# The queries' chain of the second layer, recorded at high priority, in a two-layer decoder trunk on one core

## The chip, the cores and the metric

The kernel runs on one core of one Trainium2 chip. The metric is device time in microseconds (us), the median of several runs. Of the engines, PE multiplies matrices (its weight loads are shown apart, as PEld), DVE and ACT work on vectors, POOL and SP here mostly issue transfers.

## The reference, cut to what matters

The input is a sequence of 256 tokens with 2048 features in float32. Two layers follow each other, each a pre-normalised mixer with a gate and a residual add. The first is a "forgetting" attention with 32 heads. The second, in which the change lies, is sliding-window attention with 32 query heads on 4 key heads, a rotation of the first 16 of each head's 64 features, and a sink per head:

```python
p = h @ swa_w_in[j]
q = p[..., :WQ].reshape(B, S, SWA_Q_HEADS, SWA_HEAD_DIM)
k = p[..., WQ:WQ + WK].reshape(B, S, SWA_KV_HEADS, SWA_HEAD_DIM)
v = p[..., WQ + WK:WQ + 2 * WK].reshape(B, S, SWA_KV_HEADS, SWA_HEAD_DIM)
gate = p[..., WQ + 2 * WK:]
q = partial_rope(q, pos)
k = partial_rope(k, pos)
y = swa_attention(q, k, v, swa_sinks[j])     # window 128, softmax with a sink
...
y = y * jax.nn.silu(gate)
x = x + y @ w_out
```

## The kernel before, in words

**Units and weights.** Every projection is cut into units of 256 output columns. A unit's weights come in four parts. A part is fetched by SP's queue into a raw tile `wraw` (four buffers) and split into a high and a low half, so that the product keeps nearly the full precision: ACT casts the high half (line 221) and DVE subtracts it from the raw part (line 222), both into one of five tiles `w`. PE takes a part in 16 matmuls, eight wide ones (512 columns) and eight narrow ones, 64 for a unit. Parts are taken in pairs (wide, wide, narrow, narrow), and up to five parts are loaded ahead, so a tile that PE has freed holds the part that is due three to four parts later.

**Groups.** The second layer has a unit for the keys, one for the values, and then eight groups 0 to 7, each of a query unit and a gate unit. When a unit's last matmul has been recorded, its consumer is recorded. `SwaGroup.q` is the query consumer. It has ten steps: `low_half` copies half of the accumulator on ACT (tile `half`, line 294); DVE adds the other half (`rot_t`, line 828), shuffles the result into `rot` with a mask load before it (line 830), multiplies both by the rotation's tables (lines 833, 834) and adds them (line 877); `stack_q` then splits the queries as the weights are split and lays the halves above each other (tile named `q` in the profile): two casts on ACT (line 365) and two subtractions on DVE (line 366). The tiles `rot_t`, `rot` and `q` have one buffer each.

The gate consumer is the longer one: `half` again, two DVE steps (lines 323, 324), three activations (311 to 313), a DVE step (314), one more activation (317) and a product (318). Its result is read when the group's attention output is multiplied by it.

**Attention stages.** They are not written where they run. `after` puts them down for a later count of matmul steps, and `tick`, which counts, records them between the matmuls at a high priority:

```python
def tick():
    clock[0] += 1
    for fn in due.pop(clock[0], ()):
        with tc.high_priority(HP):      # HP = 200
            fn()
```

For the second layer `SWA_DUE = ((35, 64), (52, 80), 90)`, counted from the query consumer, where one unit is 32 steps: the scores of the group's first head pair at 35, those of the second at 52, the transposition of the softmax (DVE, tile `turned`, line 466) at 64 and 80, and, in odd groups, the products with the values for two groups (tiles `psy`, `psy_s`) at 90. So the first scores of a group come just behind its gate unit, among the first matmuls of the next query unit. A score stage is six matmuls into `ps_s` that read `q`, the row maximum on DVE (lines 388, 449, 453, 888 to 891), four exponentials on ACT (line 336) and four scalings on ACT (line 355).

**What sets the order.** The matmuls stay in the order in which they are recorded. For the other engines a planner in the framework lays the order down when the program is built: whenever an engine is free in its plan, it takes, of the instructions whose inputs are there, the one with the smallest number. The number is the place in the recording; inside `tc.high_priority(200)` it is 200 smaller. From a group's query consumer to the next there are 223 recorded instructions, or 293 where the value products lie between. The order in each engine's queue is then fixed: on the chip an instruction waits behind those before it in its queue, whatever has become ready.

Before the change the stages of `tick` have the smaller numbers, and the query consumer has plain ones. So has everything else: the weight splits, the gate consumer.

Of the kernel before, what the change touches and what calls it, by code (L numbers as in the profile page):

```python
# [25 lines left out]
HP = 200  # L26
# [32 lines left out]
def trunk(  # L59
# [16 lines left out]
    nc = tc.nc  # L76
# [215 lines left out]
    def low_half(ps):  # L292
        s = work.tile([P, 2, S], F32, tag="half", name="half", bufs=HALVES)
        nc.scalar.copy(s, ps[:, :, S : 2 * S])  # L294
        return s

    def each(row):

        return row.unsqueeze(1).to_broadcast([P, 2, S])
# [61 lines left out]
    def stack_q(t):  # L361

        q2 = work.tile([P, 2, 2, S], F32R, tag="q2", name="q2", bufs=QBUFS)
        for hh, (w, other) in enumerate(((TOP, BOTTOM), (BOTTOM, TOP))):
            nc.scalar.copy(q2[w, :, hh, :], t[w])
            nc.vector.tensor_sub(q2[other, :, hh, :], t[w], q2[w, :, hh, :].bitcast(F32))  # L366
        return [q2[:, j] for j in range(2)]
# [185 lines left out]
    class FoxGroup(Group):  # L553
# [5 lines left out]
        def q(self, ps):  # L559
            t = fox.tile([P, 2, S], F32, tag="q", name="q", bufs=1)  # L560
            nc.vector.tensor_add(t, ps[:, :, 0:S], low_half(ps))
            nc.vector.tensor_mul(t, t, each(state["r08"][:, 0:S]))
            self.qT = stack_q(t)
# [260 lines left out]
    def rotate(ps):  # L824

        rr = state["rr"]
        t = swa.tile([P, 2, S], F32, tag="rot_t", name="rot_t", bufs=1)
        nc.vector.tensor_add(t, ps[:, :, 0:S], low_half(ps))
        u = swa.tile([P, 2, S], F32, tag="rot", name="rot", bufs=1)
        nc.vector.stream_shuffle(  # L830
            u.rearrange("p c s -> p (c s)"), t.rearrange("p c s -> p (c s)"), PARTNER
        )
        nc.vector.tensor_mul(t, t, each(rr[:, 0, :]))  # L833
        nc.vector.tensor_mul(u, u, each(rr[:, 1, :]))
        return t, u
# [33 lines left out]
    class SwaGroup(Group):  # L869
# [3 lines left out]
            self.u = u  # L873

        def q(self, ps):
            t, u = rotate(ps)
            nc.vector.tensor_add(t, t, u)  # L877
            self.qT = stack_q(t)

            self.attend(2 * self.u, SWA_DUE, (self.other, self) if self.u % 2 else (), True)  # L880

# [96 lines left out]
    def load_x(q):  # L978
        a, b = XP[q]

        eng = nc.scalar if q == 1 else nc.sync
        eng.dma_start(out=xT[:, a:b, :], in_=xt_d[:, a:b, :])
# [172 lines left out]
```

## Time and profile before

| | before |
|---|---|
| time, median of 3 runs | 829.42 us (829.41 to 829.52) |
| the profiled execution's own time | 828.36 us |
| its span in the profile | 826.6 us, 13821 instructions |
| PE busy | 809.6 us (98%) |
| PEld busy | 707.6 us (86%) |
| DVE busy | 633.8 us (77%) |
| ACT busy | 523.5 us (63%) |
| HBM read | 148.55 MB, 183 GB/s over the span |

The span runs from the first to the last instruction that the profiler saw on the core. A share is busy time over the span. In a timeline, a row is a start, a length, an engine, a line of the kernel, the operation, `out<-in`, the shapes and a count; a bracket holds the time the engine stood idle before the row and what ended that. Rows of the same kind that follow each other are merged into one. The second layer's groups lie between about 513 and 720 us.

### The profile page before, as it was taken

To read this page: it belongs to the slowest core of one execution; us is meant where nothing else is said; L and a number is where in the kernel's file an instruction comes from. 1 tells how busy PE (TensorE), PEld (TensorE's weight loads), DVE (VectorE), ACT (ScalarE), POOL (GpSimd) and SP (SyncE) were. 2 spreads that over 40 slices of the span, in tenths; PEclk is the share of its full clock that TensorE was granted. 3 is DMA by queue.
4 is the path that set the end of the run, shared out by engine and by line. 5 is a ranking of instruction groups with operands and counts; after the bars stand their busy time and mean duration, and the time that the engine had idled before them with its cause. 6 is when DMAs were issued, how large, how long until landed. Compare 5 with 4: busy or idle time off the path is not lost.

```text
span 826.6 us, 13821 instructions
## 1 busy us (share of the span) xinstructions
PE 809.6 (98%) x5090; PEld 707.6 (86%) x5090; DVE 633.8 (77%) x1181; ACT 523.5 (63%) x962; POOL 61.5 (7%) x102
## 2 busy tenths in 40 slices
PE   9999999999999999999999999999989989899996
PEld 7988888888888888888888888888878878788886
DVE  6988866887578866778659668699988899975655
ACT  7776674766657566575646556478667866765642
POOL 1012100100001010010003110200000000001210
PEclk9999999999999999999999999999989999999998
DMA  9766665566656565555555665955554345644642
GB/s 297 255 210 223 198 198 186 172 191 199 195 168 211 171 208 188 182 186 176 170 179 181 201 193 175 249 161 175 161 176 152 130 153 164 192 146 144 201 131 103
DMA packets 47731, 151.85 MB, mean 184 GB/s; under 512 B 5696, under 2 KB 7392, under 8 KB 47664
## 3 DMA queue, kind: packets, MB, share of 16 engines
q1 hardware_dynamic: 44640, 141.71, 53.2%
q0 software_dynamic: 1872, 7.67, 3.7%
q10 hardware_dynamic: 1152, 1.60, 0.5%
q8 instruction: 40, 0.66, 0.3%
q14 instruction: 27, 0.22, 0.1%
HBM read 148.55 MB, written 2.41 MB: 183 GB/s over the span
## 4 chain that ended last, share of the span: by engine, by line
PE 80%; DVE 8%; ACT 7%; issue 3%; DMA 2%; DVEq 0%; SPq 0%; ACTq 0%
PE acc L80 74%; DVE w L222 2%; PE ps_s L80 2%; ACT w L221 2%; PE psy L80 2%; ACT st L336 2%; PE pt L83 1%; ACT st L355 1%; DMA wraw<-in_swa_in_dram 1%; DVE q L366 1%; DVE gt L323 1%; DVE rot_t L877 0%; DVE turned L466 0%; DMA wraw<-in_vf_dram 0%; DVE rot_t L833 0%
## 5 line engine op out<-in xcount | busy, mean ns | idle before, releaser
L80 PE MATMUL acc<-xs,w 128*128 128x512 f32 (+1 forms) x2624 | 475.5, 339 | 0.0
L80 PEld LDWEIGHTS acc<-xs,w 128*128 128x128 f32 x2624 | 405.3, 190 | 53.3 <-issue 0.7
L222 DVE TENSOR_TENSOR w<-wraw,w 128x1024 fp32r<-128x1024 f32 (+4 forms) x277 | 324.6, 1180 | 114.1 <-ACT w L221 112.5
L221 ACT CAST w<-wraw 128x1024 fp32r<-128x1024 f32 (+4 forms) x277 | 276.0, 1008 | 141.4 <-PE acc L80 107.6
L80 PE MATMUL acc<-ys,w 128*128 128x512 f32 (+1 forms) x960 | 171.0, 340 | 0.0
L80 PEld LDWEIGHTS acc<-ys,w 128*128 128x128 f32 x960 | 148.7, 191 | 20.7 <-issue 0.5
L80 PE MATMUL acc<-w,xs 128*128 128x512 f32 (+2 forms) x512 | 110.3, 363 | 0.7 <-ACT w L221 0.7
L80 PEld LDWEIGHTS acc<-w,xs 128*128 128x128 f32 x512 | 86.0, 189 | 15.2 <-ACT w L221 1.2
L336 ACT ACTIVATE st<-st,mx 128x128 f32<-128x128 f32 (+1 forms) x128 | 56.6, 444 | 17.6 <-DVE mx L631 17.1
L80 PE MATMUL ps_s<-kk,q 128*128 128x256 f32 (+1 forms) x160 | 33.3, 321 | 7.4 <-DVE q L366 7.1
L294 ACT COPY half<-acc 128x512 f32<-128x512 f32 x56 | 32.6, 583 | 9.6 <-PE acc L80 9.1
L80 PEld LDWEIGHTS ps_s<-kk,q 128*128 128x128 f32 x160 | 25.2, 196 | 12.1 <-DVE q L366 9.0
L710 POOL TENSOR_TENSOR acc<-acc,sq 128x256 f32<-128x256 f32 x28 | 23.7, 848 | 89.0 <-ACT sq L704 87.9
L388 DVE CUSTOM_DVE_ANT_0 st<-ps_s,st 128x128 f32<-128x128 f32 (+1 forms) x96 | 28.2, 331 | 0.7
L311 ACT ACTIVATE gate_e<-gt 128x512 f32<-128x512 f32 x16 | 10.1, 628 | 24.7 <-DVE gt L324 24.7
L618 POOL DMA_DIRECT2D bc<-negc_d x16 | 8.9, 554 | 214.6 <-DVE st L413 143.8
L422 ACT COPY pts<-pt 128x384 f32<-128x384 f32 x32 | 15.2, 473 | 14.2 <-PE pt L83 13.8
L336 ACT ACTIVATION_READ_ACCUMULATOR st<-st,mx 128x1 f32 x128 | 24.1, 188 | 0.0
L355 ACT ACTIVATE st<-st,rl 128x128 f32<-128x128 f32 x64 | 23.9, 445 | 0.1
L155 ACT ACTIVATE xs<-xT,g_sb 128x256 fp32r<-128x256 f32 x32 | 15.5, 502 | 13.0 <-DVE xT L690 12.0
L708 POOL COPY acc<-sq 128x256 f32<-128x256 f32 x2 | 1.4, 675 | 298.9 <-ACT sq L704 298.9
L124 POOL TENSOR_SCALAR_AFFINE_SELECT bc<-bc 128x256 f32<-128x256 f32 x32 | 18.0, 585 | 73.8 <-DMA bc<-negc_d 73.8
(146 smaller groups left out, 579.1 us busy)
## 6 DMA issues: line engine op xcount, KB each, us to landing
wraw<-in_fox_in_dram SPq DMA_DIRECT2D x96, 512.0 KB, 4.5
wraw<-in_swa_in_dram SPq DMA_DIRECT2D x72, 512.0 KB, 4.7
wraw<-in_fox_out_dram SPq DMA_DIRECT2D x32, 512.0 KB, 3.9
wraw<-in_swa_out_dram SPq DMA_DIRECT2D x32, 512.0 KB, 4.4
wraw<-in_fox_in_dram SPq DMA_DIRECT2D x54, 256.0 KB, 4.4
bc<-negc_d POOLq DMA_DIRECT2D x16, 384.0 KB, 5.4
wraw<-in_vf_dram SPq DMA_DIRECT2D x4, 288.0 KB, 5.1
xT<-in_xt_dram SPq DMA_DIRECT2D x2, 512.0 KB, 8.4
```

What stands on the lines that cost most here:

```text
L80: tc.keep_in_program_order(nc.tensor.matmul(*args, **kw))
L124: return nc.gpsimd.affine_select(out=ap, in_=ap, compare_op=ALU.is_ge, fill=NEG, base=base, pattern=pattern, channel_multiplier=mult,)
L155: nc.scalar.activation(xs[:, kt, 0, :], xT[:, kt, :], AF.Copy, scale=g)
L221: state["split"] = nc.scalar.copy(high, raw)
L222: nc.vector.tensor_tensor(out=low, in0=raw, in1=high.bitcast(F32), op=ALU.subtract)
L294: nc.scalar.copy(s, ps[:, :, S : 2 * S])
L311: nc.scalar.activation(e, z, AF.Abs)
L336: nc.scalar.activation(st[:, hh, rng], st[:, hh, rng], AF.Exp, bias=nm[:, qb, hh : hh + 1], accum_out=l[:, qb, hh : hh + 1],)
L355: nc.scalar.mul(st[:, hh, rng], st[:, hh, rng], rl[:, qb, hh : hh + 1])
L388: nc.vector.tensor_tensor_reduce(out=st, in0=high, in1=st, scale=self.scale, scalar=LOWEST, op0=ALU.add, op1=ALU.max, accum_out=self.mx[:, ...
L422: nc.scalar.copy(group.new_pts(self.j, hh)[:, hh, self.j, :], pt[:, 0 : 3 * P])
L710: nc.gpsimd.tensor_add(sums[0], sums[0], s)
```

## The change

The ten steps of `SwaGroup.q` are recorded inside `tc.high_priority(HP)`, the priority that the attention stages have. The call of `attend`, which puts the stages down for later, stays outside. What is computed does not change, nor the number of instructions. `rotate` is also called for the keys, in `swa_k`; that call is as it was.

```diff
         def q(self, ps):
-            t, u = rotate(ps)
-            nc.vector.tensor_add(t, t, u)
-            self.qT = stack_q(t)
+            with tc.high_priority(HP):
+                t, u = rotate(ps)
+                nc.vector.tensor_add(t, t, u)
+                self.qT = stack_q(t)
 
             self.attend(2 * self.u, SWA_DUE, (self.other, self) if self.u % 2 else (), True)
```

## The prediction

> **What bounds the kernel now.** I read the page first (how busy each engine is), then the table of waits for the stretch in which the second layer's queries are made (500 to 745 us), then TensorE's own timeline there, and last the timeline of ACT and DVE around one of the gaps found. The page's busy line says that PE is the engine to save time on:
>
> ```profile
> PE 809.6 (98%) x5090; PEld 707.6 (86%) x5090; DVE 633.8 (77%) x1181; ACT 523.5 (63%) x962; POOL 61.5 (7%) x102
> ```
>
> So only time in which PE stands still, or runs below its clock, can be won. The table of waits (who waited for whom, us in total, times, longest) names one such wait in the second layer, and shows that the splitting of weights is not one: ACT's cast waits for PE to free a tile, and no row of the table has PE wait for `w`.
>
> ```profile
> ACT w L221 <- PE acc L80: 29.7, 17, 4.0
> PEld ps_s L80 <- DVE q L366: 9.0, 6, 3.2
> PE ps_s L80 <- DVE q L366: 7.1, 5, 2.7
> ```
>
> `ps_s<-kk,q` are the score products of a group; `q L366` is the last step of the chain that the change moves. PE's timeline (start, length, count, and in brackets the idle time before) shows which groups wait:
>
> ```profile
> 537.42 6.21 PE L80 MATMUL acc<-xs,w 128*128 128x512 f32 x34
> ...
> 567.92 13.61 PE L80 MATMUL acc<-xs,w 128*128 128x512 f32 x76
> ...
> 587.32 6.21 PE L80 MATMUL acc<-xs,w 128*128 128x512 f32 x34
> ...
> 594.08 16.44 PE L80 MATMUL acc<-xs,w 128*128 128x512 f32 x94
> 613.25 2.15 PE L80 MATMUL ps_s<-kk,q 128*128 128x256 f32 x6 [2.73 <-DVE q L366]
> 615.20 8.22 PE L80 MATMUL acc<-xs,w 128*128 128x512 f32 x34
> ...
> 643.38 6.21 PE L80 MATMUL acc<-xs,w 128*128 128x512 f32 x34
> ...
> 668.32 0.38 PE L80 MATMUL ps_s<-kk,q 128*128 128x256 f32 x1 [1.75 <-DVE q L366]
> ...
> 695.90 6.21 PE L80 MATMUL acc<-xs,w 128*128 128x512 f32 x34
> ...
> 720.86 0.38 PE L80 MATMUL ps_s<-kk,q 128*128 128x256 f32 x1 [1.99 <-DVE q L366]
> ...
> 730.35 13.72 PE L80 MATMUL acc<-ys,w 128*128 128x512 f32 x76
> ```
>
> These are groups 3, 5 and 7. What each costs is read from the repeating work. The rows at 537.42, 587.32, 643.38 and 695.90 are the same point (just behind the first scores) of groups 0, 2, 4 and 6. From 0 to 2 it takes 49.90 us, and no wait for `q` lies between; from 2 to 4 it takes 56.06, from 4 to 6 52.52. So groups 3 and 5 cost 6.16 and 2.62 us. For group 7 the second scores end the comparison: 537.42 to 567.92 is 30.50 us (group 0 to group 1), 695.90 to 730.35 is 34.45, which is 3.95 more. Together 12.73 us.
>
> That is more than the idle time, and the windows (last columns: granted clock, DMA share, GB/s) say why:
>
> ```profile
> 613.20:616.00 2.80, 2.61 (x8) 2.19 (x9) 2.74 (x4) 1.24 (x2) 0.00 (x0) 0.50 0.69 233
> 666.00:670.00 4.00, 1.91 (x11) 1.25 (x10) 3.91 (x6) 2.08 (x4) 0.00 (x0) 1.00 0.78 253
> 720.80:724.00 3.20, 2.81 (x11) 2.42 (x12) 3.10 (x8) 1.60 (x3) 0.00 (x0) 0.68 0.57 219
> ```
>
> Behind the gaps of groups 3 and 7 PE is granted 0.50 and 0.68 of its clock, behind that of group 5 all of it; 34 matmuls take 8.22 us at 615.20 where they take 6.21 elsewhere. A gap that goes takes its slow stretch with it. The Trainium skill, "TensorE: Matmul & The Clock Gate", section "Why this matters for your kernels", asks for no idle gaps over about 3 us between bursts of matmuls; by that rule groups 5 and 7, whose gaps are shorter, would cost their idle time alone, and the sum would be smaller by what group 7 lost to its clock. The trace agrees for group 5 (1.00) and not for group 7 (0.68 behind an idle time of 1.99); the comparison of periods contains what was really lost, so the sum goes by it.
>
> **The change part by part.** Group 3 shows what the chain waits behind, in the timeline of ACT and DVE:
>
> ```profile
> 598.42 1.04 ACT L221 CAST w<-wraw 128x1024 fp32r<-128x1024 f32 x1
> ...
> 599.36 0.40 ACT L336 ACTIVATE st<-st,mx 128x128 f32<-128x128 f32 x1
> ...
> 601.23 0.62 ACT L317 ACTIVATE gate_e<-gate_e 128x512 f32<-128x512 f32 x1
> ...
> 601.83 1.50 ACT L355 ACTIVATE st<-st,rl 128x128 f32<-128x128 f32 x4
> ...
> 603.23 0.56 ACT L294 COPY half<-acc 128x512 f32<-128x512 f32 x1
> 603.35 0.98 DVE L466 STREAM_TRANSPOSE turned<-st 128x768 f32<-128x768 f32 x1 [0.78 <-ACT st L355]
> 603.69 2.95 ACT L221 CAST w<-wraw 128x1024 fp32r<-128x1024 f32 x3
> 604.26 0.65 DVE L828 TENSOR_TENSOR rot_t<-acc,half 128x512 f32<-128x512 f32 x1
> 604.83 1.21 DVE L222 TENSOR_TENSOR w<-wraw,w 128x1024 fp32r<-128x1024 f32 x1
> ...
> 605.97 0.73 DVE L830 STREAM_SHUFFLE rot<-rot_t 128x512 f32<-128x512 f32 x1
> 606.60 1.20 DVE L222 TENSOR_TENSOR w<-wraw,w 128x1024 fp32r<-128x1024 f32 x1
> 607.73 0.68 DVE L833 TENSOR_TENSOR rot_t<-rot_t,rope_c 128x512 f32<-128x512 f32 x1
> ...
> 608.33 0.68 DVE L834 TENSOR_TENSOR rot<-rot,rope_c 128x512 f32<-128x512 f32 x1
> 608.93 1.21 DVE L222 TENSOR_TENSOR w<-wraw,w 128x1024 fp32r<-128x1024 f32 x1
> 609.17 0.58 ACT L294 COPY half<-acc 128x512 f32<-128x512 f32 x1
> ...
> 610.07 0.68 DVE L877 TENSOR_TENSOR rot_t<-rot_t,rot 128x512 f32<-128x512 f32 x1
> ...
> 610.78 1.26 ACT L365 CAST q<-rot_t 64x512 fp32r<-64x512 f32 x2
> 611.80 0.68 DVE L323 TENSOR_TENSOR gt<-acc,half 128x512 f32<-128x512 f32 x1
> 612.51 1.41 DVE L366 TENSOR_TENSOR q<-rot_t,q 64x512 fp32r<-64x512 f32 x2
> ```
>
> No instruction is added or removed. Per group ten move forward in the ordering: on ACT the copy `half` and two casts (0.56 + 1.26 = 1.82 us), on DVE add, shuffle with its mask load, two products, add and two subtractions (0.65 + 0.73 + 0.68 + 0.68 + 0.68 + 1.41 = 4.83 us). None is a DMA, and POOL's queue is passed by none. SP's queue is touched only through DVE: a raw buffer is free when its subtraction (L222) is done.
>
> *The start.* The copy at 609.17 is that of the gate unit and starts as that unit ends. At 6.21/34 = 0.183 us a matmul the 64 matmuls of the gate unit before it began at about 597.4 (an estimate), so `half` of the q unit was ready about then and ran at 603.23, 5.8 us late. In front of it on ACT: a weight cast, four exponentials, L317 and the scaling L355. Of these L317 is a gate step, recorded with no lift some 130 instructions earlier, which a lift of 200 overtakes. Exponentials and L355 are lifted themselves and recorded first, so they keep their lead. The cast at 598.42 may already have been taken when the q unit ended. So bounds of the gain at the start: 0 (the exponentials and L355 block it as now) and 603.23 - 598.42 = 4.8 us. I take the slot of L317, 603.23 - 601.23 = 2.0 us, because it alone is left by rank; DVE is idle 0.78 us before 603.35, so the add follows at once.
>
> *The way.* From `half` to the last subtraction the chain takes 613.92 - 603.23 = 10.7 us, of which its own work is about 6. Between its steps DVE takes weight subtractions of 1.2 us, three before L877. These already rank behind the chain; they slip in where a step's result isn't yet out, so priority alone doesn't forbid them. But they follow casts that ran at 603.69, behind `half`; with the chain 2 us earlier and L317 and L355 behind the copy, the first cast is some 0.6 us later than now, and the chain is 2.6 us further on. Bounds: 0 and 3 x 1.2 = 3.6 us. I take two of three, 2.4 us, and nothing for the gate's L323 (0.68).
>
> *The sum.* PE was ready for the scores at 594.08 + 16.44 = 610.52 and could start at 613.25. Start and way, 2.0 + 2.4 = 4.4 us, cover the 2.73 of group 3, the 1.75 of group 5 and the 1.99 of group 7, with about 1.7 us to spare in the worst. So all 12.73 us go, of which I keep back 0.4 us for a second subtraction that comes as PE arrives. The profiled execution took 828.36 us (span 826.6) and would take about 816.0; the median of the runs is 1.06 above that execution, so 817.0.
>
> *What is pushed back.* L317 and L318 end a gate that is read only after the value products, half a group later or more: nothing. The weight splits are what could cost. A w tile freed by PE is due again after three to four parts of 16 matmuls, 8.8 to 11.7 us at 0.183 each. The cast at 603.69 fills a tile freed at about 597.4; its subtraction ends at 606.04 and is due at 609.1, 3.0 us later. That is the cover, and a pushed subtraction delays the raw buffer's next DMA alike. If the whole chain (4.83) went before it, PE would wait 1.8 us; I expect less than 3.0 of pushing, since steps and subtractions go on alternating, and take 0. In the other groups, where `q` is in time, the chain moves up by at most a subtraction and gains nothing. The transposition `turned` of the group before now ranks behind the chain; in group 4 the nearest rows are
>
> ```profile
> 635.36 0.97 DVE L466 STREAM_TRANSPOSE turned<-st 128x768 f32<-128x768 f32 x1
> ...
> 637.51 0.34 PE L80 MATMUL psy_s<-turned,vr 32*64 32x128 f32 x4
> ```
>
> with 637.51 - 636.33 = 1.18 us of cover. One chain step ahead of it (0.7) fits, both subtractions (1.41) would cost 0.2 us a time, three times: 0.6 us at most, taken as 0.
>
> **The rivals.** *In part.* The start gains its 2.0 us and the way nothing, or the way one subtraction and the start nothing. The first leaves 0.73 us in group 3 and 0.3 us or so in each of the three from the second subtraction: about 2 of 12.73, so 818.7. The second leaves 1.5, 0.55 and 0.8 us of idle, and behind the largest perhaps a lower clock again (group 3 lost 6.16 - 2.73 = 3.4 us beyond its idle time before): 4 to 6 us left, 820.7 to 822.7. For it speaks that the subtractions in between already rank lower; against it, that their casts ran at 603.69, behind the copy.
>
> *No change.* The exponentials and L355 outrank the copy before and after, and L317 goes where it goes: order and time stay, 829.4. Against it: L317 carries no lift, and at 601.23 the copy had been ready for some 3.8 us.
>
> *Slower, by weights.* The chain goes whole before the split that is due first, and PE waits 4.83 - 3.0 = 1.8 us for `w` in each of the eight groups: 14.6 us against 12.73 won, so about 831.3. It decides from 1.6 us a group on, that is when the chain pushes the split by 4.6 us or more. For it: DVE stands between two rows of the fence above for no more than 0.78 us. Against it: ACT waits for PE to free tiles 17 times in this stretch, never PE for a split.
>
> **How the numbers follow.** All gone or nearly: 0.56, 817.0, by itself 815.8 to 818.3. In part: 0.25, 818.7 to 822.7. No change: 0.08. Slower by weights, or by weights with the gaps kept: 0.11. A measurement of this kernel can tell about 0.2%, 1.7 us, from no change. The first two are faster by more, 0.81; 0.08 the same; 0.11 slower. The range holds the first two with the upper end of the second and an estimate's error on either side, 815.4 to 823.5, and leaves out 0.19.
>
> **What would show it.** The waits of PE for `q L366` at groups 3, 5 and 7 gone, and periods from group 2 to 4 and 4 to 6 near 49.9 us; `half` ahead of L317 on ACT; fewer than three weight subtractions between L828 and L877; a clock of 1.00 through 613 to 724. Wrong: the same order on ACT and DVE; rows of PE waiting for `w` or `turned`; or PE idle as long for another releaser at the same places.

## The result and the profile after

The changed kernel takes 818.3 us (median of 4 runs, 816.71 to 819.01) against 829.47 us before; the ratio of the two means is 0.9857, 95% interval 0.9836 to 0.9878, so 1.4% faster. The forecast was 817.0, range 815.4 to 823.5. The profiled execution took 819.01 us, the longest of the four, with a span of 817.2 us.

PE is busy for less time and for a larger share:

```profile
PE 805.2 (99%) x5090; PEld 703.5 (86%) x5090; DVE 631.6 (77%) x1181; ACT 522.6 (64%) x962; POOL 61.2 (7%) x102
```

In the table of waits of the same stretch, 500 to 745 us, the wait for the queries has shrunk from 9.0 and 7.1 us to 0.8 and 0.3. A small new one has come, for the product at L951 (L950 before; lines behind the edit are one higher). No row of the table has PE or PEld wait for `w`:

```profile
ACT w L221 <- PE acc L80: 15.0, 9, 3.6
...
PEld ps_s L80 <- DVE q L366: 0.8, 2, 0.5
...
PE ps_s L80 <- DVE gt L951: 0.7, 1, 0.7
...
PE ps_s L80 <- DVE q L366: 0.3, 1, 0.3
```

PE's timeline has the points from which the prediction worked out its periods:

```profile
539.43 6.21 PE L80 MATMUL acc<-xs,w 128*128 128x512 f32 x34
...
589.34 6.21 PE L80 MATMUL acc<-xs,w 128*128 128x512 f32 x34
...
612.38 0.88 PE L80 MATMUL ps_s<-kk,q 128*128 128x256 f32 x6
613.09 6.21 PE L80 MATMUL acc<-xs,w 128*128 128x512 f32 x34
...
639.25 6.21 PE L80 MATMUL acc<-xs,w 128*128 128x512 f32 x34
...
689.56 0.95 PE L80 MATMUL ps_s<-kk,q 128*128 128x256 f32 x6 [0.69 <-DVE gt L951]
690.35 6.21 PE L80 MATMUL acc<-xs,w 128*128 128x512 f32 x34
...
713.76 0.86 PE L80 MATMUL ps_s<-kk,q 128*128 128x256 f32 x5 [0.31 <-DVE q L366]
...
721.01 13.72 PE L80 MATMUL acc<-ys,w 128*128 128x512 f32 x76
```

From group 0 to 2 it takes 49.91 us as before, from 2 to 4 49.91 (56.06 before), from 4 to 6 51.10 (52.52), and the last piece 30.66 (34.45). Against 49.90, 49.90 and 30.50 that is a loss of 1.37 us where it was 12.73. Group 3 has no gap left, and its 34 matmuls behind the scores take 6.21 us where they took 8.22. The granted clock (third number from the end) is 1.00 behind the scores of groups 3 and 7, where it was 0.50 and 0.68:

```profile
613.00:640.00 27.00, 27.00 (x267) 23.93 (x266) 24.81 (x58) 18.38 (x43) 0.00 (x0) 1.00 0.57 179
...
713.00:724.00 11.00, 10.69 (x66) 9.43 (x65) 10.44 (x28) 6.73 (x17) 0.00 (x0) 1.00 0.71 232
```

So 11.4 us were won here. The two spans differ by only 9.4 us, because the point at 539.43 was at 537.42 before: 2.0 us went earlier, in the first layer and the keys and values, where the order of instructions is the same. Over the runs the medians differ by 11.2.

Why the gap of group 3 is gone is seen on ACT and DVE:

```profile
600.48 1.03 ACT L221 CAST w<-wraw 128x1024 fp32r<-128x1024 f32 x1
...
601.42 0.40 ACT L336 ACTIVATE st<-st,mx 128x128 f32<-128x128 f32 x1
...
603.28 0.56 ACT L294 COPY half<-acc 128x512 f32<-128x512 f32 x1
...
603.88 1.50 ACT L355 ACTIVATE st<-st,rl 128x128 f32<-128x128 f32 x4
603.88 0.69 DVE L828 TENSOR_TENSOR rot_t<-acc,half 128x512 f32<-128x512 f32 x1
...
604.61 0.75 DVE L830 STREAM_SHUFFLE rot<-rot_t 128x512 f32<-128x512 f32 x1
605.28 0.62 ACT L317 ACTIVATE gate_e<-gate_e 128x512 f32<-128x512 f32 x1
605.40 0.98 DVE L466 STREAM_TRANSPOSE turned<-st 128x768 f32<-128x768 f32 x1
605.80 2.94 ACT L221 CAST w<-wraw 128x1024 fp32r<-128x1024 f32 x3
606.31 0.65 DVE L833 TENSOR_TENSOR rot_t<-rot_t,rope_c 128x512 f32<-128x512 f32 x1
606.88 0.68 DVE L834 TENSOR_TENSOR rot<-rot,rope_c 128x512 f32<-128x512 f32 x1
607.48 0.68 DVE L318 TENSOR_TENSOR gt<-gt,gate_e 128x512 f32<-128x512 f32 x1
608.08 0.68 DVE L878 TENSOR_TENSOR rot_t<-rot_t,rot 128x512 f32<-128x512 f32 x1
608.68 1.22 DVE L222 TENSOR_TENSOR w<-wraw,w 128x1024 fp32r<-128x1024 f32 x1
608.80 1.26 ACT L365 CAST q<-rot_t 64x512 fp32r<-64x512 f32 x2
609.93 1.40 DVE L366 TENSOR_TENSOR q<-rot_t,q 64x512 fp32r<-64x512 f32 x2
```

The copy now stands right behind the exponentials, in the place that L317 had, and L355 and L317 follow it. The three casts come behind L317, so between the first add (L828) and the second (L878) there is no weight subtraction at all where there were three. One stands behind L878, as before. The chain ends at 611.33, before PE wants the scores at 612.38.

The copy came 2 us late for an instruction of 0.62 us because L317 did not block alone. When L317 took ACT at 601.23, the scalings L355, which rank above the copy, still waited for their reciprocal. By the end of L317 at 601.85 that was there, and they went first too. The row before the change, on DVE:

```profile
601.55 0.18 DVE L352 RECIPROCAL rl<-l 128x4 f32<-128x4 f32 x1
```

### The profile page after: what moved, and what is told of

It is laid out like the page before. It is cut to its first block, busy times and chain, and to the rows that moved or that the text cites. A ratio compares the mean times of both kernels' runs of the same rounds, so it can differ in the third digit from the quotient of the medians.

```text
span 817.2 us, 13823 instructions
## 1 busy us (share of the span) xinstructions
PE 805.2 (99%) x5090; PEld 703.5 (86%) x5090; DVE 631.6 (77%) x1181; ACT 522.6 (64%) x962; POOL 61.2 (7%) x102
## 4 chain that ended last, share of the span: by engine, by line
PE 80%; DVE 7%; ACT 5%; DMA 3%; issue 3%; SPq 1%; DVEq 0%; ACTq 0%
PE acc L80 74%; DVE w L222 3%; DMA wraw<-in_fox_in_dram 2%; PE ps_s L80 2%; PE psy L80 2%; ACT w L221 1%; PE pt L83 1%; ACT st L336 1%; ACT st L355 1%; DMA wraw<-in_vf_dram 1%; SPq L208 0%; DVE ssq L995 0%; DVE turned L466 0%; DVE q L366 0%; DVE xs L156 0%
## 5 line engine op out<-in xcount | busy, mean ns | idle before, releaser
L509 ACT CAST ys<-gt 128x512 fp32r<-128x512 f32 x16 | 9.5, 619 | 24.4 <-DVE gt L955 16.2
L355 ACT ACTIVATE st<-st,rl 128x128 f32<-128x128 f32 x64 | 23.9, 445 | 1.3 <-DVE rl L352 1.1
```

The lines of the kernel that those rows point to most:

```text
L355: nc.scalar.mul(st[:, hh, rng], st[:, hh, rng], rl[:, qb, hh : hh + 1])
```

## The experiments

The theory: the gain begins at one place, on ACT, where the copy overtakes the gate's L317; the weight subtractions then drop out of the chain because their casts come later (theory 1). The rival: what counts is that the DVE steps and the casts of the chain rank above the weight splits (theory 2). The measure is the loss of the three periods, with 12.73 us before. Read in the same way from each kernel's PE timeline, with the period from group 0 to 2 beside it. Each ratio is taken to runs of the kernel before that were measured beside that kernel (medians of 829.30 to 830.18 us):

| kernel | time, us | ratio to before (95%) | 0 to 2 | 2 to 4 | 4 to 6 | 6 to 7 | loss of the three |
|---|---|---|---|---|---|---|---|
| before | 829.42 | | 49.90 | 56.06 | 52.52 | 34.45 | 12.73 |
| the change | 818.3 | 0.9857 (0.9836 to 0.9878) | 49.91 | 49.91 | 51.10 | 30.66 | 1.37 |
| copy alone | 820.56 | 0.9872 (0.9849 to 0.9896) | 51.00 | 50.14 | 51.20 | 31.58 | 2.62 |
| all but the copy | 828.81 | 0.9984 (0.9968 to 0.9999) | 49.91 | 52.54 | 54.10 | 34.50 | 10.84 |
| lift of 77 | 829.01 | 0.9978 (0.9960 to 0.9995) | 50.54 | 55.85 | 52.52 | 34.48 | 12.55 |
| odd groups alone | 822.13 | 0.9890 (0.9872 to 0.9908) | 49.91 | 51.63 | 52.42 | 30.65 | 4.40 |
| gate set back | 818.89 | 0.9870 (0.9841 to 0.9898) | 49.91 | 49.90 | 50.98 | 31.62 | 2.20 |
| lift of 400 | 818.32 | 0.9858 (0.9832 to 0.9885) | 51.29 | 49.91 | 49.90 | 30.10 | -0.39 |
| values at 86 | 818.22 | 0.9859 (0.9835 to 0.9884) | 49.93 | 50.92 | 50.89 | 30.26 | 1.77 |
| change again | 818.15 | 0.9859 (0.9836 to 0.9883) | 49.90 | 50.01 | 51.19 | 30.68 | 1.58 |
| 200, then 400 | 816.49 | 0.9840 (0.9823 to 0.9856) | 49.91 | 49.91 | 49.92 | 30.09 | -0.38 |
| change, third | 819.24 | 0.9871 (0.9850 to 0.9891) | 50.01 | 50.80 | 51.17 | 30.69 | 2.36 |

The loss is below zero with the lift of 400 since the piece from group 6 to the scores of group 7 takes 30.10 us undisturbed, 0.40 less than the piece from group 0 to 1 that stood in for it. By that, group 7 had cost 4.35 us before, not 3.95. By the intervals of the ratios, the runs from 0.9857 to 0.9872 can't be told from each other; what differs between them is read from the profiles.

**The copy alone.**

Against the kernel before, with `rotate` taking the copy as an argument:

```diff
         def q(self, ps):
-            t, u = rotate(ps)
+            with tc.high_priority(HP):
+                half = low_half(ps)
+            t, u = rotate(ps, half)
             nc.vector.tensor_add(t, t, u)
             self.qT = stack_q(t)
```

> Only the copy `half` of the query consumer is lifted by 200, the other nine steps are plain. Theory 1 (the gain begins where the copy overtakes the gate's L317 on ACT, and the weight subtractions fall out of the way because their casts come later): the copy runs right behind the exponentials of the group before, the waits for q L366 in groups 3, 5 and 7 shrink to under 0.7 us each, and of the 12.73 us that the three groups lost against the undisturbed period at most 3 are left; about 818 to 820 us. Theory 2 (the lift of the DVE steps and of the casts over the weight splits carries it): 9 us or more of the 12.73 stay, 826 us or more.

2.62 of 12.73 us are left, as theory 1 expects. The time, 820.56 us, is a little above its range, since another 1.1 us are lost in the period before, which the measure leaves out. In group 3 the copy stands ahead of L317, as with the full change:

```profile
603.00 0.56 ACT L294 COPY half<-acc 128x512 f32<-128x512 f32 x1
...
605.00 0.62 ACT L317 ACTIVATE gate_e<-gate_e 128x512 f32<-128x512 f32 x1
```

The chain ends at 612.19, after 9.2 us, where the full change takes 8.05: the other nine steps' lift is worth about 1.1 us of the chain in group 3. Its absence shows as small waits for `q` (at most 0.62 us of PE at a time) in groups 1, 5 and 7.

**All but the copy.** The same edit the other way round: `half` recorded plain, the rest lifted.

> The nine steps behind the copy are lifted by 200, the copy itself is plain. Theory 1: the copy stays behind L317 and L355 on ACT, DVE still meets the casts' subtractions, and 6 to 12 us of the 12.73 stay: 823 to 829 us. Theory 2: 3 us or less stay, 818 to 820 us.

10.84 us are left, as theory 1 expects; theory 2 falls. PE waits at the same three places. In groups 3, 5 and 7 DVE takes the steps and the weight subtractions in the same order as before: the lift of the nine steps moved nothing there. Only in group 3 is PE's wait shorter, 1.76 us against 2.73, because the copy ran 1.0 us earlier behind the point of group 2 (603.60 - 588.69 = 14.91 us against 15.91). This run also has the clock's part by itself (PE's timeline, then the windows with the granted clock as the third number from the end):

```profile
613.65 0.39 PE L80 MATMUL ps_s<-kk,q 128*128 128x256 f32 x1 [1.76 <-DVE q L366]
...
615.07 6.21 PE L80 MATMUL acc<-xs,w 128*128 128x512 f32 x34
...
666.18 0.39 PE L80 MATMUL ps_s<-kk,q 128*128 128x256 f32 x1 [1.76 <-DVE q L366]
...
667.60 7.79 PE L80 MATMUL acc<-xs,w 128*128 128x512 f32 x34
```

```profile
613.60:617.00 3.40, 3.02 (x15) 2.49 (x16) 3.31 (x9) 1.81 (x3) 0.00 (x0) 1.00 0.53 201
...
666.20:671.00 4.80, 4.47 (x15) 3.49 (x16) 4.70 (x15) 1.90 (x3) 0.00 (x0) 0.65 0.57 169
```

Behind the same idle time, 1.76 us, the 34 matmuls took 6.21 us in group 3 and 1.58 us more in group 5. The period with group 3 lost 2.64 us, that with group 5 4.20.

**A lift of 77.** `high_priority(77)` in place of `high_priority(HP)`. In the order as the planner lays it down, 77 leaves the copy behind the gate's L317 and 80 (not run) carries it past. So by rank the gate lies some 78 instructions back, not 130 as the prediction counted. That would fit a count in which instructions recorded inside a lift are left out, which no run here tests.

> All ten steps are lifted, by 77 in place of 200. That is the largest lift that leaves them behind the gate steps of the group before; the weight splits recorded last and the transposition recorded later are overtaken. Theory 1: the copy in the odd groups stays where it was, all three waits stay, 10 to 13 us of the 12.73 are left: 826 to 830 us. Theory 2 (ranking above the weight splits is what counts): 3 us or less are left, 818 to 820 us.

12.55 us of 12.73 are left, with 2.56 us of idle PE in group 3. There the order on ACT and on DVE is that of before, with L317 and the scalings ahead of the copy:

```profile
602.98 0.61 ACT L317 ACTIVATE gate_e<-gate_e 128x512 f32<-128x512 f32 x1
...
604.98 0.56 ACT L294 COPY half<-acc 128x512 f32<-128x512 f32 x1
```

A higher rank that stops short of the gate wins next to nothing (0.18 us); the gate is what had to be overtaken.

**The gate set back.** To test the blocker from the other side, the query consumer is as before the change, and the gate's last two steps rank 100 lower in the second layer (`...` stands for lines left out; behind the edit, line numbers are one higher, so L317 is L318 here):

```diff
-    def silu(z):
+    def silu(z, late=0):
...
-        nc.scalar.activation(e, e, AF.Exp)
-        nc.vector.tensor_mul(z, z, e)
+        with tc.high_priority(late):
+            nc.scalar.activation(e, e, AF.Exp)
+            nc.vector.tensor_mul(z, z, e)
...
-            silu(g)
+            silu(g, -100 if isinstance(group, SwaGroup) else 0)
```

> The query consumer as before the change, plain. Instead the last two gate steps of the second layer (the activation at L317 and the product at L318 of the listings) are set back by 100 in the ordering, so that they rank behind the copy. Theory 1 (L317 is what the copy has to overtake): the copy runs right behind the exponentials of the group before, as in the changed kernel, and at most 4 us of the 12.73 are left, like the 2.6 of the run with the copy lifted alone; 819 to 822 us. Rival (the chain needs a rank of its own): 9 us or more are left, 826 us or more.

Without any lift of the queries 10.5 of the 12.73 us are gone, at 818.89 us. In group 3 the copy stands ahead of the activation:

```profile
601.59 0.57 ACT L294 COPY half<-acc 128x512 f32<-128x512 f32 x1
...
604.53 0.62 ACT L318 ACTIVATE gate_e<-gate_e 128x512 f32<-128x512 f32 x1
```

That shows L317 as the instruction behind which the copy, and with it PE, had waited. The product L318 of the listings was set back too, but it runs on DVE, where it had ended at 602.57 in group 3, ahead of the copy.

**Odd groups alone.** `high_priority(HP if self.u % 2 else 0)`.

> Lifted by 200 in groups 1, 3, 5 and 7 alone; groups 0, 2, 4 and 6 plain. Theory 1: the three waits sit in odd groups and go as with the full change, about 818 us. The new wait of 0.69 us in group 6 (scores behind the product L951, which stands behind two weight subtractions on DVE) comes from group 6's own lift and goes: the period from group 4 to 6 falls from 51.10 to 49.9 us, about 1 us less than the full change. Rival: that wait comes from elsewhere (the PE being early) and stays, then 51 us as before it.

The odd groups' waits go, as expected. The second half of the expectation fails, and so does its rival: the wait for the score bank grows, and there are two of them.

```profile
639.58 0.95 PE L80 MATMUL ps_s<-kk,q 128*128 128x256 f32 x6 [1.49 <-DVE gt L951]
...
692.00 0.95 PE L80 MATMUL ps_s<-kk,q 128*128 128x256 f32 x6 [1.93 <-DVE gt L951]
```

The scores and the value products share the one bank pair of `ps_s`; L951 reads it for the gate. DVE's timeline at group 6 shows L951 directly behind the plain query chain, which ends late:

```profile
688.32 0.70 DVE L878 TENSOR_TENSOR rot_t<-rot_t,rot 128x512 f32<-128x512 f32 x1
...
689.70 1.39 DVE L366 TENSOR_TENSOR q<-rot_t,q 64x512 fp32r<-64x512 f32 x2 [0.69 <-ACT q L365]
691.10 0.76 DVE L951 TENSOR_TENSOR gt<-psy_s,gt 128x256 f32<-128x256 f32 x2
```

Before the change the even groups were just as plain and had no wait for the bank. What differs is that PE no longer stalls in the odd groups. The likely reading, which is argued and not shown, is that the stalls had given DVE the time to keep up. Once they are gone the lift of the even groups is worth 1.73 + 2.52 - 1.20 = 3.05 us.

**A lift of 400.** `high_priority(400)`.

> All ten steps lifted by 400 in place of 200, so that they also overtake the exponentials and scalings of the group before. Theory 1: the start comes up to 2 us earlier still, but PE waits for q by only 0.3 us a time after the change, so there is nothing left to win there: what the three periods lose stays between 0.5 and 2.5 us (1.37 with a lift of 200), 817 to 820 us. Rival a: earlier is better, the loss goes to about 0. Rival b: the transposition `turned` comes late and PE waits for it at the value products, a loss above 3 us, 821 us or more.

From group 2 on nothing is lost (rival a), so the 0.5 to 2.5 us of the theory were too much. But 1.39 us go on the way to group 2, where PE stands idle 1.27 us before the value products (`psy_s`) at 585.25. The profile names no releaser there; the transposition that they read ends at 585.16, behind steps of the lifted chain (rival b, in one place). The time is that of the change.

**The values earlier.** `SWA_DUE = ((35, 64), (52, 80), 86)`.

> The change, and the value products recorded 4 steps earlier (86 in place of 90, about 1.5 us). Theory: the score bank is read by the product L951 before the next scores want it, the wait in group 6 (0.69 us of PE) goes, and the loss falls from 1.37 to under 0.5 us: about 1 us less than the changed kernel, 817.3 us. Rival: the transposition is not yet done at the earlier place, PE waits there instead, and the loss is 1.4 us or more.

The rival held, with 1.77 us lost: the bank wait is gone, and PE waits for the transposition instead, in groups 4 and 6.

```profile
631.95 0.34 PE L80 MATMUL psy_s<-turned,vr 32*64 32x128 f32 x4 [0.92 <-DVE turned L466]
...
682.85 0.34 PE L80 MATMUL psy_s<-turned,vr 32*64 32x128 f32 x4 [0.89 <-DVE turned L466]
```

**The change again.**

> The changed kernel once more, beside the others. About 818 us; the three periods lose 1.0 to 1.7 us again; the point behind the first scores of group 0 lies anywhere from 537 to 540 us, as it has varied in the profiles so far with the same order of instructions before it.

1.58 us and 818.15 us: the remainder repeats.

**200 up to group 2, then 400.** `high_priority(2 * HP if self.u > 2 else HP)`.

> A lift of 200 in groups 0 to 2, as in the change, and of 400 from group 3 on. With 400 everywhere the periods from group 2 on lost nothing, but 1.39 us went at the value products in group 2, where PE waited for the transposition; with 200 everywhere groups 0 to 2 lost nothing. Theory: each keeps what it had, the three periods lose 0.3 us or less together and the period from group 0 to 2 is 49.9 us; 1.3 us less than the change in the profile, about 817 us, which the medians can hardly tell from the change. Rival: the plan of the later groups hangs on that of the earlier ones, and a loss of 1 us or more shows up at another place.

The first three groups and the last five each keep the better of the two. PE's timeline has no idle time before any score:

```profile
539.32 6.21 PE L80 MATMUL acc<-xs,w 128*128 128x512 f32 x34
...
589.23 6.21 PE L80 MATMUL acc<-xs,w 128*128 128x512 f32 x34
...
639.14 6.21 PE L80 MATMUL acc<-xs,w 128*128 128x512 f32 x34
...
689.06 6.21 PE L80 MATMUL acc<-xs,w 128*128 128x512 f32 x34
...
719.15 13.72 PE L80 MATMUL acc<-ys,w 128*128 128x512 f32 x76
```

At 816.49 us (815.6 to 817.17) it beats the kernel before, and it is 2.7 us below the change, which was run beside it on the same chip. Part of that is that the change lost more in this run than in its others (2.36 us against 1.37 and 1.58).

**The change, a third time, beside that.**

> The changed kernel beside it, with more rounds: 818.2 us, and 1.4 to 1.6 us lost in the three periods.

That run took 819.24 us (817.89 to 819.72), a little above the forecast, and lost 2.36 us, since the bank wait was there in group 4 too (0.65 us).

## Why the prediction was right, point by point

*Where the time is lost.* Three waits in groups 3, 5 and 7, 12.73 us by the periods. Right in place; the undisturbed last piece shows that group 7's term was 0.40 us too small.

*The start.* Forecast: the copy takes the slot of L317, 2.0 us. Measured from the period's point, it ran 603.23 - 587.32 = 15.91 us behind it before and 603.28 - 589.34 = 13.94 after: 1.97 us. The lift of 77 and the gate set back show that this slot is the cause. The working was off by its count of instructions (130 for some 78); a lift of 200 passes both. The working also said that L355 keeps its lead. It falls behind the copy, since its reciprocal is not there yet when the copy takes the slot, and the 2.0 us are L317 and L355 together.

*The way.* Forecast: two of three subtractions fall out, 2.4 us. The chain shortened from 10.69 to 8.05 us, 2.64. All three left the stretch before L878, and so did the gate's L323 (0.68), for which nothing was taken. In their place the transposition (0.98) and the gate's L318 (0.68) slip in between the steps. So the reason was right, casts that come later, but that 2.64 is so near to 2.4 is partly luck.

*The sum.* Forecast 12.73 less 0.4. Measured 11.36 by the same periods. The step that failed is "In the other groups ... the chain moves up by at most a subtraction and gains nothing", taken with no cost there. The period from group 4 to 6 loses 1.20 us: 0.3 at group 5's scores, which still wait a little for `q` (from the point of group 4 to that of 5 it takes 663.27 - 639.25 = 24.02 us, from 2 to 3 it takes 23.75), and 0.9 at group 6's scores, which wait for the score bank. The rows of the cause are DVE's two weight subtractions before L951:

```profile
686.39 2.36 DVE L222 TENSOR_TENSOR w<-wraw,w 128x1024 fp32r<-128x1024 f32 x2
688.67 0.75 DVE L951 TENSOR_TENSOR gt<-psy_s,gt 128x256 f32<-128x256 f32 x2
```

In that group's score wait the cover counted was the transposition's; the bank's reader was not counted. This is a wait that took the place of one removed, a tenth of its size. The run with the odd groups alone shows that the lift of the even groups does gain, once PE is early: without it PE waits 1.49 and 1.93 us for the bank, where it waits 0.69 with it.

*What is pushed back.* Taken as 0 for the weights, and no wait of PE for `w` appears in this stretch. The cover shrank: ACT's casts wait for PE 9 times for 15.0 us where they waited 17 times for 29.7. The rival of late weights had no hold. The rival of part of the gain came close to one of its two cases when only the copy was lifted: 2.62 us left against "about 2". Its other case, the start gaining nothing, was priced too low: 4 to 6 us left, where 10.84 are left with the copy plain, since the subtractions then stay too.

*The clock.* The full-speed clock came back as the gaps went, as the sum by periods assumed. The rule of the Trainium skill, "TensorE: Matmul & The Clock Gate", section "Why this matters for your kernels", puts the limit at idle gaps of about 3 us; the 8.22 us behind an idle time of 2.73 us and the 7.79 us behind one of 1.76 us, against 6.21 undisturbed, show that a shorter gap can cost clock too. The 2.73 us of group 3 are also below the rule's 3 us, which the prediction said of groups 5 and 7 alone.

## What to carry to other kernels

When an engine waits for a chain, look for the chain's first step, and see in its engine's queue which instruction stands in front of it without need; one such instruction (0.62 us of ACT) cost PE some 10 us here, over three groups. Here a lift in the planner's order paid only past the instruction that blocked: try a number on either side of it. When a stall goes, recheck every buffer that the stalled engine shares with others, since they may lose time that the stall had given them.

## What the hardware showed beyond expectation

Idle times of PE of 1.75 to 2.0 us cost clock in some cases and not in others: behind 1.75 and 1.76 us, 34 matmuls took 6.20 to 6.21 us three times and 7.79 once; behind 1.99 us (group 7) 7.28, 7.29 and 7.56, where 6.01 is undisturbed; behind 2.56 and 2.73 us 8.19 and 8.22. But behind the 1.93 us in which PE waited for the score bank (odd groups alone, group 6) they took 6.21, at a granted clock of 1.00. So the length of the gap alone does not decide it between 1.75 and 2.0 us; what does stays open.

The point behind the first scores of group 0 lay between 537.42 and 539.83 us in the twelve profiles. Between the kernels that share the order of instructions up to there that spread is no effect of the change, and the before profile happened to be the earliest; single spans of this kernel can't be compared more finely than about 2 us.
